# A float32 diffusion trunk on one core: normed rows at one home, gated rows at another, four weight slots at four addresses

## The chip, the cores and the metric

The kernel runs on one core of one Trainium2 chip. Its time is the device time of the program in microseconds (us), the median of three runs. A profile of one further execution goes with it; its times count from the first instruction of that execution (its span). The engines are called as in the profile: PE multiplies matrices, PEld is PE's loading of the stationary operand (weights), DVE, ACT and POOL work on vectors, SP issues the transfers from memory (DMA).

## The reference

Two layers work on 256 latent tokens and 256 context tokens of width 1024. Each layer is a half-step SwiGLU, a mixer with one input and one output projection, and a second half-step SwiGLU. Every sublayer begins with an RMS norm that is modulated by rows made from the condition.

```python
for l in range(DEPTH):                       # DEPTH = 2
    lat = lat + 0.5 * ml[2] * _swiglu(_modulate(lat, ...), w1, w3, w2)
    cx = cx + 0.5 * mc[2] * _swiglu(_modulate(cx, ...), w1, w3, w2)
    ...                                      # mixer: w_in, gated heads, w_out
    lat = lat + 0.5 * ml[8] * _swiglu(_modulate(lat, ...), w1, w3, w2)
    if not last: cx = cx + 0.5 * mc[8] * _swiglu(...)
return _rmsnorm(lat, norm_final_g)

def _swiglu(h, w1, w3, w2):                  # 1024 -> 2816 -> 1024
    return (jax.nn.silu(h @ w1) * (h @ w3)) @ w2
```

All numbers are float32.

## The kernel before

**Products.** Weights and rows are split into a high part (rounded to the type float32r) and a low part (the rest). `mm3` makes each product of three matmuls into the same PSUM bank: high weights by high rows (L287), high weights by low rows (L288), low weights by high rows (L289). There are 3076 such triples, 9228 matmuls.

**Weights.** They come in pieces of up to four 128-row tiles by 256 columns, 4096 bytes of each partition (`plan` has the order; 363 pieces). `pump` loads a piece into one of three `wraw` buffers, then ACT rounds it into `whi` (L188) and DVE subtracts it into `wlo` (L192). `whi` and `wlo` have four slots each, taken in turn: a piece of four tiles serves 24 matmuls for one span of tokens (two column halves, four tiles, three products), then PE goes on with the next slot. A tile of a piece is 1024 bytes apart from the next and a column half 512 bytes, so that within a slot every load of 128 weights (512 bytes of each partition) begins at the same address modulo 512.

**Rows.** The normed rows `h_hi` and `h_lo` are two buffers for the whole kernel. `home(at)` sets where in them the rows begin: `at` numbers of 4 bytes behind the buffers' start. The rows of one 128-feature tile take 2048 bytes (512 tokens), so that every read of 512 or of 256 tokens begins at the same address modulo 512. The home is 80 numbers (320 bytes) up to the end of the up-projections of the second layer's first SwiGLU, and 0 from there on (`self.home(0)` in `ffn`). The gated rows `g_hi`, `g_lo` of a SwiGLU are allocated anew in each `ffn`; a lead of 128 numbers (`both`, all 512 tokens) or 48 (the last SwiGLU, 256 tokens) goes ahead of `g_hi`, and its size also moves `g_lo`, which lies behind it.

**Which operand is which.** In `fm` (SwiGLU, `w_out` and most of `w_in`) the weights are the stationary operand, which PEld loads 128 columns at a time, and the rows are the moving one, streamed 512 or 256 tokens at a time. In `tm_unit` (units i and v of `w_in`) it is the other way round: rows are loaded, and 256 columns of a weight slot are streamed.

**Order.** Program order on each engine is written out by hand. PE runs one stream of matmuls; `tick` puts the mixer's small matmuls and the next norm between them. `pump` splits a piece as soon as a slot is free, so ACT and DVE wait for PE to finish a slot.

The start addresses modulo 512, of the built programs (bytes of a partition):

| | before | in it |
|---|---|---|
| `whi`, all four slots | 64 | |
| `wlo`, all four slots | 64 | |
| normed rows, home 80 | 320 | layer 0, and layer 1's first up-projections |
| normed rows, home 0 | 0 | the rest of layer 1 |
| gated rows, `both` | 320 | three SwiGLUs |
| gated rows, last SwiGLU | 0 | |

Of the kernel before, what the change touches and what calls it, by code (L numbers as in the profile page):

```python
# [10 lines left out]
F32 = mybir.dt.float32  # L11
F32R = mybir.dt.float32r
# [5 lines left out]
P = 128  # L18
# [11 lines left out]
EPS = 1e-6  # L30
POS_THETA = 10000.0
NLEV = 7
SHIFT = 80

COL = {"u": 0, "v": 512, "q": 1024, "f": 1536, "b": 2048, "i": 2560, "g": 3072}
LAT = (0, SEQ)
# [37 lines left out]
class Trunk:  # L74
# [28 lines left out]
    def plan(self):  # L103
# [28 lines left out]
        for l in range(DEPTH):  # L132
            ws += ffn(l, 1, True) + mixer(l) + out(l) + ffn(l, 2, l + 1 < DEPTH)
# [23 lines left out]
    def pump(self):  # L157
        nc = self.nc
        moved = True
        while moved:  # L160
            moved = False
            if self.n_load >= 4 and self.a_load < min(len(self.adas), self.a_done + self.N_ADA):
                it = self.adas[self.a_load]
                _, l, j, half, k = it.key
                c0 = j * D + 512 * half
                it.raw = self.wp.tile([P, 512], F32, tag="ada", name="wada", bufs=self.N_ADA)
                nc.sync.dma_start(it.raw, self.io["w_ada"][l, k * P:(k + 1) * P, c0:c0 + 512])
                self.a_load += 1
                moved = True
            if self.n_load < min(self.cap_load, len(self.ws), self.n_split + self.N_RAW):  # L170
                it = self.ws[self.n_load]
                _, name, l, k0, nk, c0 = it.key
                it.raw = self.wp.tile([P, 4, 256], F32, tag="raw", name="wraw", bufs=self.N_RAW)
                src = self.io[name][l, k0 * P:(k0 + nk) * P, c0:c0 + 256]
                nc.sync.dma_start(it.raw[:, :nk, :], src.rearrange("(k p) c -> p k c", p=P))
                self.n_load += 1
                moved = True
            if self.n_split < min(self.cap_split, self.n_load, self.n_done + self.N_SPLIT):
                it = self.ws[self.n_split]
                nk = it.key[4]  # L180
                it.hi = self.wp.tile([P, 4, 256], F32R, tag="hi", name="whi", bufs=self.N_SPLIT)
                it.lo = self.wp.tile([P, 4, 256], F32R, tag="lo", name="wlo", bufs=self.N_SPLIT)
                self.split(it.hi[:, :nk, :], it.lo[:, :nk, :], it.raw[:, :nk, :])
                self.n_split += 1
                moved = True

    def split(self, hi, lo, src):
        self.nc.scalar.activation(hi, src, AF.Copy)  # L188
        self.low(hi, lo, src)
# [95 lines left out]
    def mm3(self, ps, l_hi, l_lo, r_hi, r_lo, start, stop, swap=False):  # L285
        mm = self.nc.tensor.matmul
        mm(ps, lhsT=l_hi, rhs=r_hi, start=start, stop=False)  # L287
        mm(ps, lhsT=l_hi, rhs=r_lo, start=False, stop=False)  # L288
        mm(ps, lhsT=l_lo, rhs=r_hi, start=False, stop=stop)  # L289
# [113 lines left out]
    def ffn(self, l, n, both):  # L403
        nc = self.nc
        tc = self.tc
        w1, w3, w2 = (f"ffn{n}_w{i}" for i in (1, 3, 2))
        tokens = T if both else SEQ
        j0 = 0 if n == 1 else 6
        whole = BOTH if both else LAT
        with tc.tile_pool(name=f"g{l}{n}", bufs=1) as gp:  # L410
            lead = 128 if both else 48
            g_hi = gp.tile([P, lead + FT * tokens], F32R, tag="g_hi", name="g_hi")[:, lead:]
            g_hi = g_hi.rearrange("p (f t) -> p f t", t=tokens)
            g_lo = gp.tile([P, FT, tokens], F32R, tag="g_lo", name="g_lo")

            silu = {}

            def gate(h, p, span, part):
                for j in range(2):
                    f = 2 * p + j  # L420
                    hi, lo = g_hi[:, f, span[0]:span[1]], g_lo[:, f, span[0]:span[1]]
                    ps = h[j][:, :span[1] - span[0]]
                    if part == 1:
                        silu[j] = self.sp.tile([P, 512], F32, tag="silu", name="silu", bufs=2)[:, :span[1] - span[0]]
                        nc.scalar.activation(silu[j], ps, AF.Silu)  # L425
                    else:
                        nc.vector.tensor_tensor(silu[j], silu[j], ps, op=ALU.mult)  # L427
                        self.split(hi, lo, silu[j])

            def up(p, span, its, keep=False):  # L430
                for part, w in ((1, w1), (3, w3)):
                    h = [self.bank(), self.bank()]
                    for i, k0 in enumerate((0, 4)):
                        it = its[part, k0] if its and not keep else self.take(w, l, k0, 256 * p)
                        self.fm(it, h, self.h_hi, self.h_lo, span, KT)
                        if keep:
                            its[part, k0] = it
                        else:
                            self.done(it)
                    gate(h, p, span, part)  # L440

            if self.begun:
                hs = self.begun
                self.begun = None
                for part, w in ((1, w1), (3, w3)):
                    it = self.take(w, l, 4, 0)
                    self.fm(it, hs[part], self.h_hi, self.h_lo, BOTH, KT)
                    self.done(it)
                    gate(hs[part], 0, whole, part)
            elif both:  # L450
                its = {0: None}
                up(0, LAT, its, keep=True)
                self.drain()
                up(0, CTXC, its)
            else:
                self.drain()
                up(0, LAT, None)
            for p in range(1, FF // 256):
                up(p, whole, None)

            if (l, n) == (DEPTH - 1, 1):
                self.home(0)

            def down(p, span):
                ps = [self.bank(), self.bank()]
                for k0 in range(0, FT, 4):
                    it = self.take(w2, l, k0, 256 * p)
                    self.fm(it, ps, g_hi, g_lo, span, FT)
                    self.done(it)
                self.update(l, j0 + 2, p, ps, span)  # L470

            for p in range(3):
                down(p, whole)
            down(3, LAT)
            if n == 1 or l + 1 < DEPTH:
                nl, nj = (l, 3) if n == 1 else (l + 1, 0)
                self.behind(self.norm(nl, nj, 0, NF[0]))
                if both:
                    down(3, CTXC)
                    self.drain()  # L480
                    self.behind(self.norm(nl, nj, 1, NF[1]))
# [367 lines left out]
    def start(self):  # L849
# [12 lines left out]
        for s in range(2):  # L862
            nc.vector.memset(self.sel[:, s, s:s + 1], 1.0)
        self.x = cp.tile([P, KT, T], F32, tag="x", name="x")
        self.h_all = [cp.tile([P, KT * T + n], F32R, tag=f"h_{w}", name=f"h_{w}")
                      for w, n in (("hi", 256), ("lo", 128))]
        self.home(SHIFT)
        self.ssq = cp.tile([P, T], F32, tag="ssq", name="ssq")
        self.mods = cp.tile([P, DEPTH * N_MOD, 2, KT], F32, tag="mods", name="mods")
# [3 lines left out]
        with self.tc.tile_pool(name="start", bufs=1) as st:  # L873
# [144 lines left out]
            for part in (1, 3):  # L1018
# [5 lines left out]
                it = self.take(f"ffn1_w{part}", 0, 0, 0)  # L1024
# [62 lines left out]
```

## Time and profile before

| | us |
|---|---|
| median of three runs | 1797.11 (1796.61 to 1797.27) |
| the profiled execution, device time | 1796.01 |
| its span, first to last instruction | 1794.2 |
| DVE busy in it | 1130.4 |
| ACT busy in it | 670.6 |

A row of the grouped view reads: line, engine, operation, result<-operands, partitions by elements, number of instructions, busy us, mean ns of one, idle us of the engine just before them and what ended the idle time. In rows of PE the operand that is streamed stands first, the loaded one second. A matmul's own duration runs until its result has come out at the far end, and the next one starts long before that; what a matmul costs the stream is the distance from its start to the next start, called its step here. In a view by stretches, "x" counts every instruction of which any part lies in the stretch; so the mean step of a stretch that holds matmuls of one form alone is its length plus one duration, divided by the count.

### The profile page before, as it was taken

The numbers are of one execution on the slowest core, as the hardware profiler recorded it, in microseconds if no ns is written. First come the engines' busy times: TensorE is split into PE (matmuls) and PEld (weight loads), VectorE is DVE, ScalarE is ACT, GpSimd is POOL, SyncE is SP. The second block draws the span as 40 slices with busy tenths as digits, with TensorE's granted clock in tenths as the row PEclk, the third lists the DMA queues.
The fourth block names the chain that finished last, engine by engine and source line by source line (L and its number), as shares of the span: only waits on it lengthen the run. The fifth ranks groups of instructions, "written<-read, shape, count | busy, mean of one in ns | idle before, by whom it ended". The sixth has DMA issues, their size and how long they took to land. (4 is left out here: it accounts for less than half of the span.)

```text
span 1794.2 us, 27050 instructions
## 1 busy us (share of the span) xinstructions
PE 1763.5 (98%) x10853; PEld 1544.1 (86%) x10853; DVE 1130.4 (63%) x1746; ACT 670.6 (37%) x1087; POOL 19.6 (1%) x26
## 2 busy tenths in 40 slices
PE   7999999999999999999999999999999999989998
PEld 5788888899899899888888898888888989979998
DVE  4876676775736667666666676555545677665554
ACT  3422222236535444222222252222222465545543
POOL 0000000000000000000000000000000000000000
PEclk8999999999999999999999999999999999989999
DMA  8565555654222124555555545555554532446663
GB/s 314 165 176 161 179 160 166 182 187 133 71 60 83 59 59 135 148 163 158 149 157 159 176 136 153 159 159 154 157 171 153 159 106 83 130 120 197 193 188 127
DMA packets 230645, 266.65 MB, mean 149 GB/s; under 512 B 10368, under 2 KB 192376, under 8 KB 230520
## 3 DMA queue, kind: packets, MB, share of 16 engines
q1 hardware_dynamic: 230520, 264.93, 48.5%
q8 instruction: 85, 1.39, 0.3%
q14 instruction: 40, 0.33, 0.1%
HBM read 263.84 MB, written 1.05 MB: 148 GB/s over the span
## 5 line engine op out<-in xcount | busy, mean ns | idle before, releaser
L287 PE MATMUL mm<-h_hi,whi 128*128 128x512 f32 (+1 forms) x2016 | 705.5, 350 | 5.0 <-ACT h_hi L384 3.0
L288 PE MATMUL mm<-h_lo,whi 128*128 128x512 f32 (+1 forms) x2016 | 698.4, 346 | 1.3 <-DVE h_lo L373 1.0
L289 PE MATMUL mm<-h_hi,wlo 128*128 128x512 f32 (+1 forms) x2016 | 695.7, 345 | 0.0
L192 DVE TENSOR_TENSOR wlo<-wraw,whi 128x1024 fp32r<-128x1024 f32 x362 | 430.9, 1195 | 322.0 <-ACT whi L188 318.9
L188 ACT ACTIVATE whi<-wraw 128x1024 fp32r<-128x1024 f32 x362 | 371.1, 1032 | 396.5 <-PE mm L288 274.3
L287 PEld LDWEIGHTS mm<-h_hi,whi 128*128 128x128 f32 x2016 | 382.1, 190 | 56.6 <-issue 4.0
L288 PEld LDWEIGHTS mm<-h_lo,whi 128*128 128x128 f32 x2016 | 382.0, 190 | 50.8 <-DVE h_lo L373 5.5
L289 PEld LDWEIGHTS mm<-h_hi,wlo 128*128 128x128 f32 x2016 | 381.9, 189 | 47.2
L250 DVE SCALAR_TENSOR_TENSOR acc<-wada,cond,acc 128x512 f32<-128x512 f32 x392 | 275.9, 748 | 36.4 <-DMA wada<-in_w_ada_dram 34.3
L287 PE MATMUL mm<-g_hi,whi 128*128 128x256 f32 (+1 forms) x836 | 280.7, 336 | 0.0
L289 PE MATMUL mm<-g_hi,wlo 128*128 128x256 f32 (+1 forms) x836 | 277.5, 332 | 0.0
L288 PE MATMUL mm<-g_lo,whi 128*128 128x256 f32 (+1 forms) x836 | 277.5, 332 | 0.0
L287 PEld LDWEIGHTS mm<-g_hi,whi 128*128 128x128 f32 x836 | 157.9, 189 | 18.4 <-issue 2.4
L289 PEld LDWEIGHTS mm<-g_hi,wlo 128*128 128x128 f32 x836 | 158.0, 189 | 15.7
L288 PEld LDWEIGHTS mm<-g_lo,whi 128*128 128x128 f32 x836 | 158.0, 189 | 15.2
L188 ACT ACTIVATE g_hi<-silu 128x512 fp32r<-128x512 f32 (+1 forms) x92 | 51.8, 563 | 179.0 <-DVE silu L427 179.0
L425 ACT ACTIVATE silu<-mm 128x512 f32<-128x512 f32 (+1 forms) x92 | 48.2, 527 | 134.7 <-PE mm L289 130.5
L192 DVE TENSOR_TENSOR g_lo<-silu,g_hi 128x512 fp32r<-128x512 f32 (+1 forms) x92 | 55.7, 606 | 57.8 <-ACT g_hi L188 57.8
L427 DVE TENSOR_TENSOR silu<-silu,mm 128x512 f32<-128x512 f32 (+1 forms) x92 | 55.0, 598 | 28.7 <-PE mm L289 28.4
L287 PE MATMUL mm<-whi,h_hi 128*128 128x256 f32 x224 | 64.8, 289 | 0.0
L288 PE MATMUL mm<-wlo,h_hi 128*128 128x256 f32 x224 | 63.0, 281 | 0.0
L289 PE MATMUL mm<-whi,h_lo 128*128 128x256 f32 x224 | 63.0, 281 | 0.0
(128 smaller groups left out, 1055.9 us busy)
## 6 DMA issues: line engine op xcount, KB each, us to landing
wraw<-in_ffn_w_dram SPq DMA_DIRECT2D x271, 512.0 KB, 4.4
wada<-in_w_ada_dram SPq DMA_DIRECT2D x256, 256.0 KB, 2.9
wraw<-in_w_in_dram SPq DMA_DIRECT2D x56, 512.0 KB, 3.9
a<-in_w_ada_dram SPq DMA_DIRECT2D x8, 1024.0 KB, 9.9
wraw<-in_w_out_dram SPq DMA_DIRECT2D x16, 512.0 KB, 4.2
wraw<-in_ffn_w_dram SPq DMA_DIRECT2D x19, 256.0 KB, 2.7
x<-in_x_dram SPq DMA_DIRECT2D x2, 512.0 KB
ctx<-in_ctx_dram SPq DMA_DIRECT2D x2, 512.0 KB, 6.1
```

Of the source, the lines that this page charges most:

```text
L188: self.nc.scalar.activation(hi, src, AF.Copy)
L192: self.nc.vector.tensor_tensor(lo, src, hi.bitcast(F32), op=ALU.subtract)
L250: nc.vector.scalar_tensor_tensor(acc[:, s], raw, c, acc[:, s], op0=ALU.mult, op1=ALU.add)
L287: mm(ps, lhsT=l_hi, rhs=r_hi, start=start, stop=False)
L288: mm(ps, lhsT=l_hi, rhs=r_lo, start=False, stop=False)
L289: mm(ps, lhsT=l_lo, rhs=r_hi, start=False, stop=stop)
L425: nc.scalar.activation(silu[j], ps, AF.Silu)
L427: nc.vector.tensor_tensor(silu[j], silu[j], ps, op=ALU.mult)
```

## The change

Only addresses change. Both programs have 15,420 instructions, the same on every engine, in the same order and with the same waits.

```diff
-SHIFT = 80
+SHIFT = 0
+LEADW = 64
...
-                it.hi = self.wp.tile([P, 4, 256], F32R, tag="hi", name="whi", bufs=self.N_SPLIT)
-                it.lo = self.wp.tile([P, 4, 256], F32R, tag="lo", name="wlo", bufs=self.N_SPLIT)
+                it.hi = self.slot("hi")
+                if not self.n_split:
+                    self.wp.tile([P, LEADW], F32, tag="pad", name="pad")
+                it.lo = self.slot("lo")
...
+    def slot(self, part):
+        t = self.wp.tile([P, 1024 + 16], F32R, tag=part, name="w" + part, bufs=self.N_SPLIT)
+        return t[:, :1024].rearrange("p (k c) -> p k c", k=4)
...
-            lead = 128 if both else 48
+            lead = 48
...
-                      for w, n in (("hi", 256), ("lo", 128))]
+                      for w, n in (("hi", 0), ("lo", 0))]
```

The normed rows stay at their buffers' start for the whole kernel (`home(0)` in `ffn` now sets what was set before). A slot is 64 bytes longer than its piece, which puts each slot 64 bytes further modulo 512 than the one before. The pad, which nothing writes or reads, gives `wlo` the same four places as `whi`. The start addresses modulo 512 become:

| | after |
|---|---|
| `whi` and `wlo`, slots 0, 1, 2, 3 | 64, 128, 192, 256 |
| normed rows, all the time | 0 |
| gated rows, all four SwiGLUs | 256 |

Other tiles move too: the `wada`, `tmp`, `silu` buffers and the mixer's tiles by 256 bytes modulo 512 against before (`wada` and `tmp` from 64 to 320, the others from 320 to 64); `wraw`, `acc`, `x` and `ssq` stay as they were modulo 512.

## The prediction

> **What bounds the kernel now.** I read the page first, then the waits, then the groups by form, then stretches in which only one kind of matmul runs.
>
> ```profile
> PE 1763.5 (98%) x10853; PEld 1544.1 (86%) x10853; DVE 1130.4 (63%) x1746; ACT 670.6 (37%) x1087; POOL 19.6 (1%) x26
> ...
> PEclk8999999999999999999999999999999999989999
> ...
> PE mm L287 13%; PE mm L288 13%; PE mm L289 12%; PE aux L530 1%; DVE wlo L192 1%; ACT whi L188 0%; DVE tmp L383 0%; PE ada_ps L259 0%; DVE h_lo L373 0%; DMA wraw<-in_ffn_w_dram 0%; PE o L614 0%; PE aux L600 0%; PE o L610 0%; DVE x L398 0%; ACT yt L1039 0%
> ```
>
> PE is busy for 98% of the span at a granted clock of nine tenths or more nearly throughout. The chain that ended last runs through the three products of `mm3`. Next the waits:
>
> ```profile
> ACT whi L188 <- PE mm L288: 274.3, 103, 5.0
> ...
> PE mm L287 <- ACT h_hi L384: 3.0, 2, 1.9
> ```
>
> ACT waits 274.3 us in all for PE to free weight slots, while PE's waits for normed rows sum to 3.0 us and none of its waits names a weight slot. So weights are ready in time, and a nanosecond more or less on a matmul reaches the end almost whole. The matmuls of the change, by form:
>
> ```profile
> L287 PE MATMUL mm<-h_hi,whi 128*128 128x512 f32 x1184 | 469.7, 397 | 1.9 <-ACT h_hi L384 1.9
> ...
> L287 PE MATMUL mm<-h_hi,whi 128*128 128x256 f32 x832 | 235.9, 284 | 3.1 <-ACT h_hi L188 1.9 <-ACT h_hi L384 1.1
> ...
> L287 PE MATMUL mm<-g_hi,whi 128*128 128x512 f32 x396 | 156.1, 394 | 0.0
> ...
> L287 PE MATMUL mm<-g_hi,whi 128*128 128x256 f32 x440 | 124.6, 283 | 0.0
> ...
> L287 PE MATMUL mm<-whi,h_hi 128*128 128x256 f32 x224 | 64.8, 289 | 0.0
> ```
>
> L288 and L289 have as many each, so the counts go by three. Divided by the home of the rows: normed rows 512 wide 3456 at home 320 and 96 at home 0; 256 wide 768 and 1728; gated rows 512 wide 1188 at 320; 256 wide 792 at 320 and 528 at 0; `tm_unit` (last row) 384 with rows at 320 and 288 with rows at 0.
>
> What one costs depends on the home. Stretches of one kind each, in order: normed 512 at 320; gated 512 at 320; normed 256 at 320; gated 256 at 320; `tm_unit` at 320; normed 256 at 0; gated 256 at 0.
>
> ```profile
> core 0: us, PE busy (x), PEclk, DMA share, GB/s
> 698.50:725.00 26.50, 26.50 (x119) 1.00 0.55 167
> 934.20:958.00 23.80, 23.80 (x107) 1.00 0.46 147
> 649.50:662.00 12.50, 12.50 (x107) 1.00 0.29 84
> 382.20:399.00 16.80, 16.80 (x142) 1.00 0.63 205
> 509.60:520.80 11.20, 11.20 (x96) 1.00 0.33 95
> ...
> 1608.00:1724.00 116.00, 116.00 (x1026) 1.00 0.66 194
> 1725.00:1784.00 59.00, 59.00 (x523) 1.00 0.48 152
> ```
>
> With a duration of 0.39 us (512 wide) or 0.28 (256 wide) the steps are: (26.50 + 0.39) / 119 = 226 ns and the same for gated rows; 256 wide at home 320 (12.50 + 0.28) / 107 = 119.4, 120.3 and 119.6 ns; 256 wide at home 0 (116.00 + 0.28) / 1026 = 113.3 and 113.3 ns. All at full clock, with PE busy all the time. The last two stretches have more traffic than most of the slower ones (DMA share 0.66 and 0.48 against 0.29 and 0.33), so traffic is not the reason. Two kinds are short and go by single starts, first and last:
>
> ```profile
> 1452.70 0.39 PE L287 MATMUL mm<-h_hi,whi 128*128 128x512 f32 x1
> ...
> 1456.66 0.39 PE L289 MATMUL mm<-h_hi,wlo 128*128 128x512 f32 x1
> ```
>
> Seventeen steps of normed 512 at home 0 take 3.96 us, 232.9 ns each. And `tm_unit` with rows at 0, 46 steps in 5.41 us, 117.6 ns:
>
> ```profile
> 1504.31 0.28 PE L288 MATMUL mm<-wlo,h_hi 128*128 128x256 f32 x1
> ...
> 1509.72 0.28 PE L289 MATMUL mm<-whi,h_lo 128*128 128x256 f32 x1
> ```
>
> So the same instructions cost about 6.5 ns more at one home than at the other, and the good home is 320 for 512 wide and 0 for 256 wide. While a matmul streams, the load for the next one runs. I call **distance** the address of that load minus the address of the streamed rows, modulo 512. Before it takes two values in `fm`: 256 (64 minus 320) and 64 (64 minus 0); in `tm_unit` 256 and 448. Extra cost by distance: 512 wide 0 at 256, 6.5 ns at 64; 256 wide 6.5 at 256, 0 at 64, 4.3 at 448. That the distance decides, and not one address, is supported by `tm_unit`: with the roles exchanged, distance 256 gives the same 120 ns.
>
> **The change part by part.** No instruction, wait or transfer is added, removed or moved; SP's queue is untouched. The pad is space alone. DVE and ACT touch moved buffers, but have slack (63% and 37% busy): nothing, and if each of the 363 splits took a tenth longer, ACT's 274.3 us of waiting would still cover it. What counts is the distance, which now changes with the slot, a quarter of the pieces each: normed rows 64, 128, 192, 256; gated rows 320, 384, 448, 0; `tm_unit` 448, 384, 320, 256.
>
> 128, 192, 320, 384, 0, and 448 for `fm`, do not occur in a steady run of the trace. Bounds: 0 and 6.5 ns, the two ends seen. Nearest rows: 448 in `tm_unit`, +4.3; and a stretch in which the steady pattern had been broken by a small matmul:
>
> ```profile
> 111.02 0.39 PE L288 MATMUL mm<-h_lo,whi 128*128 128x512 f32 x1
> ...
> 113.33 0.39 PE L289 MATMUL mm<-h_hi,wlo 128*128 128x512 f32 x1
> ```
>
> Ten steps in 2.31 us are 231 ns, 4.5 above steady. I take **4.5 ns for every unseen distance**, nearer the dear end because both rows lie there. The trace says also that such a broken pattern needs some nine steps to settle; the change breaks it at each new slot. I add nothing for that, since 4.5 is itself the price of an unsettled run.
>
> Mean extra of normed rows in `fm`: 512 wide (6.5 + 4.5 + 4.5 + 0) / 4 = 3.9 ns; 256 wide (0 + 4.5 + 4.5 + 6.5) / 4 = 3.9. Gated rows 4.5. `tm_unit` (4.3 + 4.5 + 4.5 + 6.5) / 4 = 5.0. Against before, in us (count times the difference):
>
> - normed 512: 3456 × 3.9 = +13.4; the 96 at home 0 gain 0.3
> - gated 512: 1188 × 4.5 = +5.3
> - normed 256 from home 320: 768 × (3.9 − 6.5) = −2.0
> - gated 256 from 320: 792 × (4.5 − 6.5) = −1.6
> - normed 256 from home 0: 1728 × 3.9 = +6.7
> - gated 256 from 0: 528 × 4.5 = +2.4
> - `tm_unit`: 384 × (5.0 − 6.5) = −0.6 and 288 × (5.0 − 4.3) = +0.2
>
> Sum **+23.5 us**, on the profiled execution's 1796.0: 1819.5; the median of the runs shown lies 1.1 above it, so 1820.6. With every unseen distance free the same sum is −2.8 (1794.3); with every one at 6.5 it is +35 (1832).
>
> One rule speaks against all this. The Trainium skill, "TensorE: Matmul & The Clock Gate", Part 2 (What happens when you issue a matmul), says that PE has two independent read ports, and that "Loading the next tile's weights doesn't steal SBUF read bandwidth from the running matmul." By it no address would matter and the time would stay at 1797. The trace disagrees: 113.3 against 120 ns at full clock, told apart by the home alone.
>
> **The rivals.**
>
> *Faster: the dear pattern holds only while the distance stays the same.* The 256-wide run from 1608 to 1724 us keeps one step through some forty pieces, so PE settles into a pattern and stays. If a new distance at each piece throws PE out of the 120-ns pattern and it goes on at the cheap step, nothing is lost at 512: −6.5 × (768 + 792 + 384 + 96) − 4.3 × 288 = −14.5 us, 1782.6. It decides the sign while the 4644 matmuls 512 wide rise by less than 14.5 / 4644 = 3.1 ns on average. Against it: 232.9 ns at distance 64 is steady, and the broken pattern above got dearer, not cheaper.
>
> *Within the noise: unseen distances are all free.* Then the seen ones alone remain, −2.8 us as above, 1794.3. Or addresses do not matter at all (the rule above), 1797.
>
> *Slower, by the home alone:* home 0 costs 6.5 at 512 wide and nothing at 256, wherever the weights lie; home 256 is unseen, half of 6.5. Normed +22.5 − 5.0, `tm_unit` −0.8, gated +3.9 − 2.6 + 1.7: +19.7, 1816.8. For it: before, the weights never move, so the trace cannot separate home and distance in `fm`; against it `tm_unit`, as said.
>
> That the slots do not lie where the change says can be left out: the built program has them there.
>
> **How the numbers follow.** The sum by distance 0.58; home alone 0.12; unseen distances free 0.08; addresses without effect 0.04; patterns thrown off to the cheap step 0.18. A measurement of this kernel can tell about 0.2% (3.6 us) from no change. Slower 0.70, same 0.12, faster 0.18. Range: from 1790, which takes in the free case with its spread, to 1834, the dear bound; the faster rival is left out.
>
> **What would show it.** In the profile after, PE should stay the bound, with DVE and ACT busy for as long as before. Steps should go by the slot: quarters of the pieces with steps of 226 beside quarters at 231 to 233 in the first SwiGLU, and 113 beside 117 to 120 in the last one, where all were 113.3. The mean step from 1725 on should be near 118. Wrong: if the 512-wide steps stay at 226 in all slots, the first and largest term falls; if 256-wide steps of the last SwiGLU stay at 113, the price of unseen distances was a guess too dear; if ACT's waits for PE vanish, something else became late.

## The result, and the profile after

| | before | after |
|---|---|---|
| median of three runs, us | 1797.11 | 1812.31 (1810.22 to 1813.80) |
| the profiled execution, us | 1796.01 | 1813.80 |
| its span, us | 1794.2 | 1812.0 |

The change makes the kernel slower by 15.2 us. The ratio after to before is 1.0084, with a 95% interval of 1.0061 to 1.0107. The three runs of before all belong to the lower of two groups, some 7 us apart, into which its times fall in the runs further down.

The page after, in the same rows as before: busy times by engine, the granted clock in 40 slices, and the lines on the chain that ended last. Lines of the kernel stand 7 further down, so `mm3`'s three products are L294 to L296.

```profile
PE 1777.1 (98%) x10853; PEld 1543.8 (85%) x10853; DVE 1129.1 (62%) x1746; ACT 670.7 (37%) x1087; POOL 19.7 (1%) x26
...
PEclk8999999999999999999999999999999999999999
...
PE mm L294 13%; PE mm L295 13%; PE mm L296 12%; PE aux L537 1%; DVE wlo L199 1%; DVE tmp L390 0%; ACT whi L195 0%; PE ada_ps L266 0%; DVE h_lo L380 0%; DMA wraw<-in_ffn_w_dram 0%; PE mm L1051 0%; PE o L621 0%; PE aux L607 0%; PE o L617 0%; DVE x L405 0%
```

PE's busy time rises by 13.6 us (1763.5 to 1777.1) with the same 10,853 instructions and the same clock, while DVE, ACT and POOL stay where they were. The chain runs through the same lines. The waits of the kernel after (waiting engine, its line, what ended the wait: us in all, how often, longest):

```profile
ACT whi L195 <- PE mm L295: 281.2, 100, 5.1
...
PE ada_ps L266 <- DMA a<-in_w_ada_dram: 5.2, 3, 3.2
...
PE mm L294 <- ACT h_hi L391: 3.0, 2, 1.9
```

ACT still waits for PE (281.2 us, 274.3 before) and PE hardly waits for rows: 3.0 us in this row, as before, and 5.9 us in both kernels with two smaller rows of `h_hi` and `h_lo` (the prediction took the one row for the sum). So weights are as early as before, and the time is in the steps of the matmuls themselves. The wait of `ada_ps` for its transfers is at the start of the program, where nothing was changed. In the profile of before it was 0.8 us:

```profile
PE ada_ps L259 <- DMA a<-in_w_ada_dram: 0.8, 1, 0.8
```

It is 2.4 us in two later profiles of before, and 2.6 to 5.2 in those of the other kernels, so part of the difference is in which execution was profiled.

The steps do go by the slot. The timeline of the kernel after, first in layer 0's first SwiGLU, 512 wide, then in layer 1's last one, 256 wide (start us, duration us, engine, line, operation). The slots come round in the order 64, 256, 192, 128 (the built program's), so normed rows at 0 meet the same distances in the same order. Shown is the first matmul of a piece of 24 in each slot, and the last of the fourth.

```profile
205.15 0.40 PE L294 MATMUL mm<-h_hi,whi 128*128 128x512 f32 x1
...
210.62 0.39 PE L294 MATMUL mm<-h_hi,whi 128*128 128x512 f32 x1
...
233.67 0.39 PE L294 MATMUL mm<-h_hi,whi 128*128 128x512 f32 x1
...
239.17 0.40 PE L294 MATMUL mm<-h_hi,whi 128*128 128x512 f32 x1
...
244.76 0.39 PE L294 MATMUL mm<-h_hi,whi 128*128 128x512 f32 x1
...
250.12 0.40 PE L296 MATMUL mm<-h_hi,wlo 128*128 128x512 f32 x1
...
1737.72 0.28 PE L294 MATMUL mm<-h_hi,whi 128*128 128x256 f32 x1
...
1740.60 0.28 PE L294 MATMUL mm<-g_hi,whi 128*128 128x256 f32 x1
...
1743.32 0.28 PE L294 MATMUL mm<-g_hi,whi 128*128 128x256 f32 x1
...
1746.16 0.28 PE L294 MATMUL mm<-g_hi,whi 128*128 128x256 f32 x1
...
1748.90 0.28 PE L294 MATMUL mm<-g_hi,whi 128*128 128x256 f32 x1
```

512 wide, normed rows: distance 256 takes 5.47 us for 24 steps (205.15 to 210.62), 227.9 ns each, of which the first seven are unsettled and the rest 227. Distance 192 takes 5.50 us (from 233.67), 229.2 ns; distance 128 5.59 us, 232.9 ns; distance 64 5.36 us for 23 steps (to 250.12), 233.0 ns. Before, at home 320, all settled to 226.7 (the timeline's steps are 226 and 227 in turn; by its stretch the prediction had 226). 256 wide: 2.88 us, 120.0 ns for normed rows at distance 256; then gated rows, 2.72 us, 113.3 ns at 448; 2.84 us, 118.3 at 384; 2.74 us, 114.2 at 320. Before, all of this SwiGLU was 113.3. The stretch from 1725 us on has by the same arithmetic as before (59.00 + 0.28) / 509 = 116.5 ns a step:

```profile
core 0: us, PE busy (x) PEld busy (x) DVE busy (x) ACT busy (x) POOL busy (x), PEclk, DMA share, GB/s
1725.00:1784.00 59.00, 59.00 (x509) 59.00 (x509) 31.50 (x38) 25.78 (x33) 0.00 (x0) 1.00 0.61 189
```

All steps of a kind and a distance in the trace after, as the mean extra over the settled cheap step (226.7 ns 512 wide, 113.3 ns 256 wide; steps over 20 ns longer, which contain another matmul or a wait, left out):

| distance modulo 256 | 512 wide, normed / gated | 256 wide, normed / gated | `tm_unit` |
|---|---|---|---|
| 0 | +1.3 / +1.3 | +6.5 / +6.5 | +6.7 |
| 64 | +6.6 / +6.6 | +1.1 / +0.5 | +2.5 |
| 128 | +6.0 / +6.1 | +5.1 / +5.1 | +5.8 |
| 192 | +2.6 / +2.5 | +0.8 / +1.1 | +4.6 |

Normed rows have distances 64, 128, 192 and 256, gated rows 320, 384, 448 and 0. That the two columns agree says that the distance counts **modulo 256, not 512**: 320 costs what 64 does, 448 what 192 does, 0 what 256 does.

### The profile page after: what moved, and what is told of

Its sections match the earlier page's. It is cut to its first block, busy times and chain, and to the rows that moved or that the text cites. A ratio compares the mean times of both kernels' runs of the same rounds, so it can differ in the third digit from the quotient of the medians.

```text
span 1812.0 us, 27050 instructions
## 1 busy us (share of the span) xinstructions
PE 1777.1 (98%) x10853; PEld 1543.8 (85%) x10853; DVE 1129.1 (62%) x1746; ACT 670.7 (37%) x1087; POOL 19.7 (1%) x26
## 5 line engine op out<-in xcount | busy, mean ns | idle before, releaser
L294 PE MATMUL mm<-h_hi,whi 128*128 128x512 f32 (+1 forms) x2016 | 709.3, 352 | 4.9 <-ACT h_hi L391 3.0
L295 PE MATMUL mm<-h_lo,whi 128*128 128x512 f32 (+1 forms) x2016 | 702.4, 348 | 1.5 <-DVE h_lo L380 1.0
L296 PE MATMUL mm<-h_hi,wlo 128*128 128x512 f32 (+1 forms) x2016 | 699.3, 347 | 0.0
L195 ACT ACTIVATE whi<-wraw 128x1024 fp32r<-128x1024 f32 x362 | 370.9, 1031 | 404.8 <-PE mm L295 281.2
L294 PEld LDWEIGHTS mm<-h_hi,whi 128*128 128x128 f32 x2016 | 381.6, 189 | 60.4 <-issue 4.0
L295 PEld LDWEIGHTS mm<-h_lo,whi 128*128 128x128 f32 x2016 | 381.4, 189 | 53.5 <-DVE h_lo L380 5.4
L296 PEld LDWEIGHTS mm<-h_hi,wlo 128*128 128x128 f32 x2016 | 381.2, 189 | 50.9
L294 PE MATMUL mm<-g_hi,whi 128*128 128x256 f32 (+1 forms) x836 | 281.7, 337 | 0.0
L295 PE MATMUL mm<-g_lo,whi 128*128 128x256 f32 (+1 forms) x836 | 278.7, 333 | 0.0
L296 PE MATMUL mm<-g_hi,wlo 128*128 128x256 f32 (+1 forms) x836 | 278.1, 333 | 0.0
L294 PEld LDWEIGHTS mm<-g_hi,whi 128*128 128x128 f32 x836 | 157.4, 188 | 19.8 <-issue 2.4
L296 PEld LDWEIGHTS mm<-g_hi,wlo 128*128 128x128 f32 x836 | 157.4, 188 | 17.2
L295 PEld LDWEIGHTS mm<-g_lo,whi 128*128 128x128 f32 x836 | 157.5, 188 | 16.1
L294 PE MATMUL mm<-whi,h_hi 128*128 128x256 f32 x224 | 64.7, 289 | 0.0
L296 PE MATMUL mm<-whi,h_lo 128*128 128x256 f32 x224 | 62.9, 281 | 0.0
L295 PE MATMUL mm<-wlo,h_hi 128*128 128x256 f32 x224 | 62.9, 281 | 0.0
```

## Experiments

Where an expectation speaks of theories: A is the distance, counted modulo 256; the rivals were that the alternation of addresses itself costs (B), that the home of the rows alone decides (C), and others named where they come up. In no experiment is anything left out of the computation. "Distance" is that of normed rows unless said otherwise; an x number is the count of matmuls in a stretch.

**One address for all slots, the homes of the change.**

```diff
-        t = self.wp.tile([P, 1024 + 16], F32R, tag=part, name="w" + part, bufs=self.N_SPLIT)
+        t = self.wp.tile([P, 1024], F32R, tag=part, name="w" + part, bufs=self.N_SPLIT)
...
-                if not self.n_split:
-                    self.wp.tile([P, LEADW], F32, tag="pad", name="pad")
...
-            lead = 48
+            lead = 112
```

> The homes of the change, but all weight slots at one address (64 modulo 512), so that the distance never changes in fm: it is 64 modulo 256 everywhere. Theory A (the distance modulo 256 sets the step, at the prices read in the changed kernel): every 512-wide step 233 ns, every 256-wide step in fm 113 to 114 ns, tm_unit 118 ns; sum against before (3456 x 5.9 + 1188 x 6.0 - 768 x 6.1 - 792 x 6.6 - 384 x 2) ns = +17 us, about 1814 us. Theory B (what costs is that the address changes from slot to slot, which breaks a settled pattern): with one address the patterns settle, 512-wide steps 227 ns, and the time falls to about 1785 to 1797 us.

Measured 1815.89 us (1814.34 to 1818.33), 1.0086 times before, 1.0053 to 1.0119. Two stretches of it, 512 wide in layer 0 and 256 wide in layer 1:

```profile
core 0: us, PE busy (x), PEclk, DMA share, GB/s
707.00:733.00 26.00, 26.00 (x113) 1.00 0.55 169
1640.00:1740.00 100.00, 100.00 (x884) 1.00 0.66 193
```

The steps are (26.00 + 0.39) / 113 = 233.5 ns and (100.00 + 0.28) / 884 = 113.4 ns: distance 64 is dear 512 wide and cheap 256 wide, with nothing alternating. With one address the loss is as large as with four, so alternation is not what costs (B falls). In this kernel `wada`, `tmp`, `silu` and the mixer's tiles lie modulo 512 where they lay before, so it is not their new places either.

**Four slot addresses, the old homes.** The other half of the change alone.

```diff
-SHIFT = 0
+SHIFT = 80
...
-            lead = 48
+            lead = 64 if both else 112
...
-                      for w, n in (("hi", 0), ("lo", 0))]
+                      for w, n in (("hi", 128), ("lo", 128))]
```

> The four slot addresses of the change, but the homes of before (normed rows at 320, then 0; gated rows at 320, in the last SwiGLU at 0). The distances are then 0, 64, 128, 192 modulo 256 a quarter each, as in the changed kernel, but paired with other slots. Theory A (distance modulo 256): the same quarters of 227 to 228, 233, 233 and 229 ns, and the time of the changed kernel, 1812 us within 3. Theory C (the home of the streamed rows decides, wherever the weights lie): the steps of before, and about 1797 us. If the distance counted modulo 512 and not 256, rows at 320 with weights at 192 (distance 384) would differ from rows at 0 with weights at 128.

Measured 1811.32 us (1809.67 to 1812.68), 1.0068 times before, 1.0048 to 1.0088. The timeline of this kernel at home 320, one piece in each slot:

```profile
202.26 0.39 PE L294 MATMUL mm<-h_hi,whi 128*128 128x512 f32 x1
...
207.76 0.40 PE L294 MATMUL mm<-h_hi,whi 128*128 128x512 f32 x1
...
213.12 0.40 PE L296 MATMUL mm<-h_hi,wlo 128*128 128x512 f32 x1
...
259.46 0.39 PE L294 MATMUL mm<-h_hi,whi 128*128 128x512 f32 x1
...
265.06 0.39 PE L294 MATMUL mm<-h_hi,whi 128*128 128x512 f32 x1
...
270.28 0.39 PE L296 MATMUL mm<-h_hi,wlo 128*128 128x512 f32 x1
```

In order: 24 steps in 5.50 us, 229.2 ns, at a distance of 192 modulo 256; 23 in 5.36 us, 233.0 ns, at 128; 24 in 5.60 us, 233.3 ns, at 64; 23 in 5.22 us, 227.0 ns, at 0. The rows lie where they lay before and the same four prices come out as at home 0: the home alone does not decide (C falls). And distance 384 at home 320 costs what 128 cost at home 0, so the period of 256 holds here too.

**Distances between the multiples of 64.** Two kernels, one profiled execution each, with four other starts within slots of 1024 + 64 numbers. Normed rows stay at 0, gated rows lie at 320, which is 64 modulo 256.

```diff
+OFF = (56, 8, 24, 40)
...
+        t = self.wp.tile([P, 1024 + 64], F32R, tag=part, name="w" + part, bufs=self.N_SPLIT)
+        o = OFF[self.n_split % 4]
+        return t[:, o:o + 1024].rearrange("p (k c) -> p k c", k=4)
...
-            lead = 48
+            lead = 0
```

Distances 32, 96, 160, 224:

> Slots 0 to 3 at distances 32, 96, 160 and 224 (modulo 256) from the normed rows, 64 less from the gated rows; otherwise the changed kernel. A measurement of the price between the four points known. If the price changes smoothly, 512-wide steps of about +3 to +4, +6, +4, +2 ns over 226.7; 256-wide steps of about +4, +3, +3, +4 over 113.3. If only units of 64 bytes count, distances 32, 96, 160, 224 repeat 0, 64, 128, 192.

The same with `OFF = (52, 60, 4, 12)`, distances 16, 48, 80, 112 (gated rows 208, 240, 16, 48):

> Slots 0 to 3 at distances 16, 48, 80 and 112 (modulo 256) from the normed rows, 64 less (208, 240, 16, 48) from the gated rows; otherwise the changed kernel. A measurement of the price on a grid of 16 bytes. With units of 64 bytes, 16 and 48 cost as 0 (512 wide +1, 256 wide +6 ns) and 80 and 112 as 64 (+6.6, +1); with a smooth price, values between.

Measured 1830.55 and 1826.18 us. In the first, the mean 512-wide step of each distance costs +6.5 to +7.5 ns and the 256-wide one of `fm` +3.5 to +6.4. For 512 wide that is at or over the dear bound of the prediction, where neither a smooth course nor steps of 64 bytes had put it. In the second, normed 512-wide steps cost +5.3 to +6.6 at all four distances, gated ones +5.7 at 208, +1.1 at 240, +1.0 at 16 and +6.6 at 48. Distance 16 cost 6.1 for normed rows (modulo 256, weights at 16, rows at 0) and 1.0 for gated rows (weights at 80, rows at 64). So off the multiples of 64 the distance alone does **not** decide; what does is open.

**High and low weights at different addresses.** Is it the load under way (for the next matmul) or the matmul's own weights whose address counts? One profiled execution, high weights at distance 64, low weights at 0; the rest is as in the two kernels above.

```diff
+OFF = {'hi': 0, 'lo': 48}
...
+        o = OFF[part]
```

> High parts of the weights at distance 64 and low parts at distance 0 (modulo 256) from the normed rows, in every slot. While a matmul streams, the load for the next one runs: high weights during the first product (for the second), low weights during the second, high weights during the third. If the load under way is what collides (theory A): 512-wide steps of normed rows 233, 227 to 229, 233 ns for the first, second and third product. If a matmul's own weights decide (theory D): 233, 233, 227.

Measured 1822.51 us. The timeline of this kernel; L293, L294 and L295 are the three products:

```profile
715.28 0.39 PE L293 MATMUL mm<-h_hi,whi 128*128 128x512 f32 x1
715.50 0.40 PE L294 MATMUL mm<-h_lo,whi 128*128 128x512 f32 x1
715.74 0.39 PE L295 MATMUL mm<-h_hi,wlo 128*128 128x512 f32 x1
715.97 0.39 PE L293 MATMUL mm<-h_hi,whi 128*128 128x512 f32 x1
```

All three steps are between 220 and 240 ns, and their means over the trace are 230.9, 233.0 and 233.2 ns. Neither the second nor the third product got cheap, as A and D each wanted of one of them. A stream in which one load in three is at a cheap distance stays dear (2 ns less so in the first product); which load it is stays open. The gated rows of this kernel, at 64, tell something more: their high weights are at distance 0 and their low ones at 192, and 512 wide the three products take 229.3, 230.6 and 233.3 ns, a mean of +4.4, where each of the two distances kept for a whole piece costs +1.3 and +2.5. So the prices of the table are those of a stream that keeps its distance, and cannot be added up load by load.

**A good distance for each width.** The table says what to do: 512 wide wants 0, 256 wide 64. Most pieces are used at one width, so a slot of 1024 + 64 numbers can begin where its piece needs it, with the homes fixed. `width` gives the tokens over which a piece's loads are streamed, 0 for `tm_unit`.

```diff
+OFF = {512: 48, 256: 0, 0: 32}
...
+        t = self.wp.tile([P, 1024 + 64], F32R, tag=part, name="w" + part, bufs=self.N_SPLIT)
+        o = (OFF[self.width(*key[1:4], key[5])] + 16 * key[1].endswith("w2")) % 64
+        return t[:, o:o + 1024].rearrange("p (k c) -> p k c", k=4)
```

> Homes never move, and a piece is put in its slot by the width of the rows that it will be used with: 512 wide at distance 0 (modulo 256), 256 wide at distance 64, tm_unit with its rows 64 ahead of the streamed weights. Theory A (distance modulo 256): 512-wide steps stay at 227 to 228 ns, 256-wide steps go from 120 to 114 in layer 0 and stay at 113 to 114 later, tm_unit falls to about 116; against before -768 x 5.5 - 792 x 5.5 - 384 x 4 - 288 x 2 - 96 x 6 ns = -11 us, about 1786 us, faster than both kernels. Theory B (a change of address from piece to piece costs by itself): the pieces change address in layer 0 at each change of width, some of the gain is lost there, 1790 us or more.

And the same with 256 wide at distance 192 (`256: 32`):

> As the run sorted by width, but 256-wide pieces at distance 192 instead of 64. Theory A: distance 192 cost 0.8 ns over the floor at 256 wide in the changed kernel, against 1.1 at 64, so the two are alike within 1 us, about 1786 us.

The first took 1791.80 us, 0.9967 times before (0.9953 to 0.9981): faster than both kernels, but some 6 us less so than expected. The second took 1799.03, 1.0009 (0.9998 to 1.0020): a miss. In both the 512-wide steps are at 227; the shortfall is in the 256-wide ones, which in the second are at 117.8 in nearly every piece that no small matmul breaks. The first kernel's last stages, normed rows up to some 1721 us and gated rows behind:

```profile
core 0: us, PE busy (x), PEclk, DMA share, GB/s
1600.00:1700.00 100.00, 100.00 (x851) 1.00 0.64 185
1725.00:1775.00 50.00, 50.00 (x427) 1.00 0.56 175
```

The steps are (100.00 + 0.28) / 851 = 117.8 and (50.00 + 0.28) / 427 = 117.8 ns, at the distance that cost 113.3 before and in the kernel with one address. Its ten times lie in two groups, 1790.1 to 1791.9 and 1794.8 to 1795.9; the profiled execution, at 1795.7, is of the upper one. That led to a further theory (E): at one and the same distance a 256-wide stream can run in either of **two lasting patterns**, 113.3 or 117.8 ns, and what it came from decides which.

**Is it the program or the execution?** The same kernel profiled again, and before twice more.

> The run sorted by width, unchanged, profiled once more: its ten times fell into two groups, 1790.1 to 1791.9 and 1794.8 to 1795.9 us, and the profile had one of the second group, with 117.8 ns a step from about 1600 us to the end. Theory E: an execution of the first group has steps of 113.3 ns in a part of that stage; 4.5 ns on some 900 of the 1600 steps are 4 us. Otherwise both groups have 117.8 there, and the difference lies elsewhere.

It took 1791.54 us, and the same two stretches are:

```profile
core 0: us, PE busy (x), PEclk, DMA share, GB/s
1600.00:1700.00 100.00, 100.00 (x882) 1.00 0.65 190
1725.00:1775.00 50.00, 50.00 (x427) 1.00 0.52 164
```

113.7 ns where the other execution of the same program had 117.8, and 117.8 behind, as there. Some 1,040 steps of normed rows from 1600 us on at 4.1 ns are 4.3 us, and the two executions lie 4.2 us apart. Both executions ran at 113 ns from about 1575 to 1587 us. There the stream stops for some 7 us, in which PE does small matmuls of the next norm and waits, and the steps behind it are 213 to 640 ns long until about 1600 us (granted clock 0.53 and 0.68 in 1590 to 1600 us, 1.00 and 0.98 in the 12 us behind); one execution came out of it in the dear pattern, the other in the cheap one. Each stayed in it up to the gated rows, where the second fell into the dear one too. So the two patterns exist at the same addresses of the same program.

> The kernel before, unchanged, profiled once more: its times fall into two groups, near 1796 and near 1804 us. Theory E (two lasting patterns at 256 wide): an execution near 1804 shows steps of 117.8 ns in the last stage, from about 1600 us to the end, where the first profile had 113.3; 4.5 ns on some 1600 steps are 7.2 us. An execution near 1796 shows 113.3 there. Otherwise: an execution near 1804 shows 113.3 there, and the difference lies elsewhere (the clock, the start).

> The same once more, so that the other group may be seen; the same expectations.

Before's times fall in two groups as well: in the 47 runs of it beside the timed experiments, 1794.7 to 1799.2 and 1801.6 to 1805.5 us. The two executions took 1794.51 and 1796.79, both of the lower group, and both had the cheap step there. The first:

```profile
core 0: us, PE busy (x), PEclk, DMA share, GB/s
1640.00:1740.00 100.00, 100.00 (x885) 1.00 0.65 193
```

That is 113.3 ns, and the second has one matmul fewer. No profile caught the upper group. Some 7 us would be 4.5 ns on the 1,600 steps of the last stages, but that before's upper group is the 117.8-ns pattern is argued, not shown.

**Throwing the stream out of the pattern.** Under E, a change of distance between two cheap ones might bring the stream to the cheap pattern. 256-wide pieces alternately at distances 64 and 192, the rest as in the kernel by width; and another kernel, with `NARROW = (48, 0, 0, 0)`, has one 256-wide piece in four at distance 0 and the others at 64.

```diff
+NARROW = (0, 32, 0, 32)
...
+        w = self.width(*key[1:4], key[5])
+        o = (OFF[w] + (NARROW[self.n_split % 4] if w == 256 else 0) + 16 * key[1].endswith("w2")) % 64
```

> As the run sorted by width, but 256-wide pieces lie in turn at distance 64 and 192. The run sorted by width showed two lasting patterns at one and the same distance, 113.3 and 117.8 ns a step. Theory E (PE keeps the pattern that it fell into until something disturbs it, and a change of distance from piece to piece lets it fall anew; in the changed kernel each piece at 64 or 192 reached 113 to 114 ns within a few steps of its start): 256-wide steps of 113.5 to 115 ns throughout and 1782 to 1785 us. Theory F (the pattern depends on something else, such as the clock dip ahead of the last stage): 117.8 ns in whichever stretch it happens, and 1790 us or more.

> As the run sorted by width, but one 256-wide piece in four lies at distance 0 and the others at 64. Theory E: the pieces at 0 cost 120 ns a step, and each piece after one starts anew and falls to 113 to 114 ns, a mean of about 115.5 ns over the 256-wide steps and 1786 to 1788 us. Theory F: pieces at 64 stay at 117.8 ns in some stretches in spite of the piece at 0, and 1792 us or more.

The alternating kernel took **1789.28 us** (1786.95 to 1790.88), 0.9939 times before, 0.9920 to 0.9957. Before fell in both of its groups beside it, and all six runs of the alternating kernel lie at least 3.6 us under the lowest time of before in any experiment (1794.51). Its last SwiGLU, then that of the other kernel:

```profile
core 0: us, PE busy (x), PEclk, DMA share, GB/s
1620.00:1690.00 70.00, 70.00 (x620) 1.00 0.65 191
```

```profile
core 0: us, PE busy (x), PEclk, DMA share, GB/s
1640.00:1740.00 100.00, 100.00 (x847) 1.00 0.62 183
```

113.4 ns in the first, and 118.4 in the second, which took 1800.59 us, 1.0001 times before (0.9986 to 1.0015). In that one the quarter at distance 0 costs 120 and the pieces at 64 behind it 117.8: (120 + 3 × 117.8) / 4 = 118.4. That is what F had forecast for this kernel, not E: a change of distance does not by itself bring the cheap pattern. Which change it is matters: a stream at distance 64 is cheap behind 192 in the alternating kernel (53 of the 57 such pieces that nothing breaks) and behind 128 in the kernel after (all 31; the one at 1746.16 begins with steps of 117, 123 and 118 and goes on at 113), and dear behind 0 in the other kernel (all 29). One case speaks against a plain rule: in the three profiles of before the first normed piece at 64, near 1421 us, follows gated ones at 0 and is cheap. The alternating kernel is 4 to 7 us over its expectation; most of `tm_unit` (480 to 520 us, about 1500 us), whose distance does not alternate, and the first pieces of some other stretches are still near 117.8.

## Why the prediction was right, and where it was off

The direction, the mechanism and the range held: 1812.31 in 1790 to 1834, slower. The range is so wide that no change at all would have lain in it; it is the steps by slot that speak for the mechanism. The rise was 15.2 us where 23.5 was forecast. The terms, as sums of all steps of a kind from one matmul of `mm3` to the next, in the two profiled executions:

| term | predicted | measured |
|---|---|---|
| normed 512, both homes | +13.1 | +11.4 |
| gated 512 | +5.3 | +4.1 |
| normed 256 (−2.0 and +6.7) | +4.7 | +0.9 |
| gated 256 (−1.6 and +2.4) | +0.8 | −1.0 |
| `tm_unit` | −0.4 | −0.4 |
| sum | +23.5 | +15.0 |

The remaining 2.8 us of the span's 17.8 lie outside these steps; the wait of `ada_ps` at the start alone is 4.4 longer.

- **What bounds the kernel** was read rightly: PE, with ACT waiting for it. A nanosecond on a matmul arrived at the end: of the 17.8 us between the two profiled executions 15.0 are in the steps (that the medians lie 15.2 apart is close to that by chance). The pieces number 362, not 363, which changes nothing.
- **That the distance decides** held on the multiples of 64: one address at the new homes gave 233.5 and 113.4 ns, four addresses at the old homes gave the same four prices as at the new ones. Between these multiples it does not hold, as the distances of 16 show.
- **"I take 4.5 ns for every unseen distance"** is the step that was mis-sized. Of the unseen distances, 512 wide 128 and 384 cost 6.0, 320 6.6, 192 and 448 2.5, and 0 only 1.3; 256 wide 128 and 384 cost 5.1, but 192, 320 and 448 only 0.5 to 1.1, and 0 6.5. 512 wide the dear and the cheap ones nearly cancel (a mean of 4.1 against 3.9 normed, 4.5 gated); 256 wide the mean is 3.4 and 3.3 against 3.9 and 4.5, over 3816 steps. No 512-wide distance costs near 4.5, so that the largest terms came out within 2 us is luck: the prediction's nearest row, a stream settling behind a small matmul, was no price of a distance. The mean step from 1725 us on, forecast near 118, is 116.5.
- **The row of normed 256** holds something besides price. Where the stream stops ahead of the last SwiGLU, both executions go on for some us at a lower granted clock (0.72 in 1600 to 1612 us before, in 1612 to 1624 us after), and the steps over 133 ns from 1560 us on cost 8.5 us more than cheap ones before and 6.9 us after. Without steps that long the row is about +2.6, not +0.9, against the +4.7 forecast.
- **The period was taken as 512**, for which nothing in the trace spoke. By a period of 256 the rows of before would have priced two of the distances called unseen, 0 (as 256) and 320 (as 64), both ways: 0 and 6.5 ns 512 wide, 6.5 and 0 ns 256 wide. Both came out so within 1.3 ns.
- **A floor of zero** for the kinds taken as free before was the smaller fault: before, 512-wide steps already had a mean of 0.7 to 0.8 ns over 226.7 (settling behind small matmuls), and normed 256-wide ones at home 0 had 0.5. So +3.3 ns of the +4.1 was new.
- **"I add nothing"** for the settling at each new slot: at distance 0, 512 wide, it is the whole +1.3.

The rivals. Addresses without effect: fell. The rule of the Trainium skill, "TensorE: Matmul & The Clock Gate", Part 2, that a load of weights takes no read bandwidth from the running matmul, does not settle what a load costs these float32r streams: a step takes 233.5 or 226.7 ns by the addresses alone. Whether it is the reads of the two operands that meet, no run shows. The home alone: its 1816.8 is nearer to the measured time than the sum's 1820.6, but it fell to the four addresses at the old homes. Unseen distances all free: fell at 128 and 384, and at 320 512 wide and 0 256 wide; nearly true 256 wide at 192, 320 and 448. The faster rival, that a new distance throws PE to the cheap step: fell for this change, where 512-wide pieces at 64 and 128 are dear from end to end and 256-wide ones at 0 are at 120 within two steps. Its idea was not idle, though: the alternating kernel and the two executions of the kernel by width show that at cheap distances a 256-wide stream has two patterns, and that the distance before has a part in which.

## What to carry to other kernels

When a kernel is bound by back-to-back matmuls, compare the start-to-start step of equal instructions between stages before and after any change of layout: a difference of 3% 512 wide (233.5 against 226.7 ns) or 6% 256 wide (120 against 113.3) at full clock can come from where the loaded and the streamed operand lie, and the right offset differs with the width that is streamed. Choose the offset for each use, on a grid of 64 bytes, and test it with one kernel for each offset rather than price the unseen ones by a mean. Where the times of one program fall in two groups, profile it more than once before a reason is found in its code.

## What the runs showed of the hardware

- The step of a float32r stream goes by the difference between the address of the loaded weights and that of the streamed rows, modulo 256 (both on multiples of 64, the difference kept for a whole piece): 512 wide, 226.7 ns at 0 and about 233 at 64 and 128; 256 wide, 113.3 at 64 and 120 at 0.
- Where differences off the multiples of 64 are kept for a piece, nearly all placements tried are dear (+5.3 to +7.5 ns 512 wide), with two exceptions at about +1, and the same distance can be of either kind.
- A 256-wide stream holds one of two patterns, 113.3 or 117.8 ns, for over 100 us at the same addresses, at a granted clock of 1.00 in both; the distance of the stream before it has a part in which, but does not alone decide it. In both executions of the kernel by width the last changes of pattern came behind the pause near 1590 us or where gated rows took over from normed ones, not within a steady run.
